# An encoder block: the low part of the gates' token sums made by ScalarE and an accumulating transfer instead of VectorE

## The chip, the cores and the metric

The kernel runs on one core of one Trainium2 chip. The metric is the device time of one execution in microseconds (us); for the kernel before it is the median of the runs that were made. A core has five engines that run their own instruction streams in order and wait for each other through semaphores: TensorE (PE, with its weight loads PEld), VectorE (DVE), ScalarE (ACT), GpSimd (POOL) and SyncE (SP), which here only issues transfers. ACT and POOL can issue transfers too; such an instruction stands in the engine's stream like any other, and what stands behind it waits until it has been issued.

## The reference

One layer of an encoder block works on x, 1024 tokens by 1024 channels, in float32:

```python
u = rms_norm(x, norm1_g[l])
proj = u @ w_in[l]
q, k, v, cb, cc, ch, ga, gb = jnp.split(proj, split_pts, axis=-1)
q = rms_norm(q.reshape(B, S, N_HEADS, HEAD_DIM), q_norm_g[l])
k = rms_norm(k.reshape(B, S, N_HEADS, HEAD_DIM), k_norm_g[l])
y_a = neighbourhood_attention(q, k, v, rpb[l]) @ w_attn_branch[l]
y_b = short_gated_conv(cb, cc, ch, conv_w[l]) @ w_conv_branch[l]
merged = jax.nn.sigmoid(ga) * y_a + jax.nn.sigmoid(gb) * y_b
x = x + merged @ w_o[l]
h = rms_norm(x, norm2_g[l]) @ w_mlp_in[l]
x = x + jnp.square(jax.nn.relu(h)) @ w_mlp_out[l]
```

The gates ga and gb are 1024 channels each. Both are a plain product of u with columns of w_in.

## The kernel before

**Numbers in two parts.** Every operand of a matmul is held as two float16 tiles: a high part, the value rounded to float16, and a low part, the value minus the high part. A product takes three matmuls per 128 rows of contraction (high by high, high by low, low by high), so a unit of 8 contraction blocks is 24 matmuls into one PSUM bank.

**Stages.** The kernel computes in this order: norm of x and the v projection, the q and k projections (token blocks b = 0 to 7 each), attention with the convolution's projections between its steps, the gates and branches, the output projection, and the MLP. The gates after the first block of channels, and the MLP, use a scheme of seven products in place of eight (`seven`): operands are cut into quarters, and some products take sums or differences of quarters. For the gates those sums of the token side ("S forms") are made early, while q is projected, and parked in a DRAM buffer `GS`, to be read back transposed after attention (`turn_s`).

**How the S forms are made (`sforms`, lines 474 to 494).** xt holds the eight blocks of x, normalised in place by two ACT instructions (L482) per pair of blocks n and n+4. Four POOL operations (L486) then make the sums in place, so xt[n] and xt[n+4] become the four forms in float32. This is "form n", for n = 0 to 3. "Split n" follows: a tile s of 128 by 4 by 2 by 512 float16 (three buffers) takes the high part from ACT (L491, 2048 elements in each partition) and the low part from DVE (L493, xt minus the high part). `sform_store` then issues, on ACT's stream (L498), the transfer of the whole tile, 1 MB, to GS. The table `SFORM` sets the order, form 0, 1, 2, split 0, form 3, split 1, 2, 3, each at a mark counted in units of matmuls.

**The order of the work.** It is written out by the program itself: a unit of matmuls is emitted, then foreground generators (`fg`) and background generators (`bg`) are advanced by some steps, and each step emits instructions of DVE, ACT, POOL or SP. So the order within each engine's stream is fixed when the program is built, and on the chip only waits move it.

**What stands around the change.** The v units of blocks 3 to 7 end with an ACT copy (L516) and a DVE operation (L517). A unit of q for block b puts its product into a bank of PSUM taken in turn from tag d (three banks) and tag o (two banks); `qk_vec` then copies it out on ACT (L736), squares it (L737), sums and scales it on DVE (L740, L747), splits it (L754 on ACT, L756 on DVE), and `finish_qk` issues a transpose on SP (L767) into qD. qD takes the place of xt, so the first of these transposes waits for all readers of xt. In the background `Chunk.prep` prepares k's weights: four ACT squares (L266) give a sum, a small matmul (L201) adds it over the partitions, and then ACT makes the high parts (L306) and DVE the low parts (L297) of eight pieces. The units of the k projection need these.

Below, q0 to q7 and k0 to k7 are the units of the q and k projections by block; q0, q2, ... go to banks d, and q1, q3, ... to banks o.

Of the kernel before, what the change touches and what calls it, by code (L numbers as in the profile page):

```python
# [14 lines left out]
AF = mybir.ActivationFunctionType  # L15
OP = mybir.AluOpType
# [36 lines left out]
def encoder_block(ctx: ExitStack, tc: tile.TileContext, x, weights, cols, gqk, rel, masks, out):  # L53
    nc = tc.nc
    V, A, G, T, SP = nc.vector, nc.scalar, nc.gpsimd, nc.tensor, nc.sync
# [41 lines left out]
    def at(c, i, n=1):  # L97
        return slice(c.start + i, c.start + i + n)
# [83 lines left out]
    def apart(mark, n=3, of=units):  # L182
        while of[0] < mark + n and not forced[0]:
            yield WAIT
# [289 lines left out]
    def sforms():  # L474

        for mark, n, split in SFORM:
            yield from apart(mark, 0)
            pair = xt[:, n:n + 5:4]
            if not split:
                assert turned[0] >= n + 5  # L480
                for b in (n, n + 4):
                    A.activation(xt[:, b], xt[:, b], AF.Copy, scale=sc[:, at(ys, b)])  # L482
                z = [xt[:, b, c:c + 512] for b in (n, n + 4) for c in (0, 512)]
                for o, a, b, op in ((3, 2, 3, OP.subtract), (2, 0, 2, OP.subtract),
                                    (0, 3, 0, OP.subtract), (1, 1, 0, OP.add)):
                    G.tensor_tensor(z[o], z[a], z[b], op=op)  # L486
                continue
            v = wqk.tile([128, 4, 2, 512], F16, name="s16", bufs=3)
            v4 = v.rearrange("p (b h) w c -> p b h w c", b=2)
            f = pair.rearrange("p b (h c) -> p b h c", h=2)  # L490
            A.activation(v4[:, :, :, 0], f, AF.Copy)  # L491
            yield
            V.tensor_tensor(v4[:, :, :, 1], f, v4[:, :, :, 0], op=OP.subtract)  # L493
            fg.append(sform_store(n, v))

    def sform_store(n, v):
        yield from apart(units[0], 1)
        A.dma_start(GS[:, n], v)  # L498
        formed[0] = n + 1
# [208 lines left out]
    tick()  # L708
    fg.append(qk_gain())
    fg.append(sforms())  # L710
    step(2)
    for b in range(3, 8):
# [1231 lines left out]
```

## Time and profile before

| | |
|---|---|
| Median of 2 runs | 1206.88 us (1206.52 to 1207.23) |
| Span of the profiled execution, first to last instruction | 1205.3 us |
| PE busy | 1188.0 us, 99% of the span |
| DVE busy | 938.7 us, 78% |
| ACT busy | 759.8 us, 63% |
| POOL busy | 433.1 us, 36% |
| Transfers | 173.36 MB, mean 144 GB/s |

The profiled execution has no time of its own beside its span; what lies between the span and the median of the runs is 1.6 us, before the first and after the last instruction. The span counts from the first instruction. In a timeline each row has its start in us, its length in us, the engine, the source line, the operation, the tile written and the tiles read, the shape, how many instructions the row merges, and in square brackets how long the engine sat idle before it and what ended that. A row of ACTq or SPq is an instruction of the engine's queue, such as the issue of a transfer. In the table of waits the three numbers are the total, the number of times and the longest.

### The profile page before, as it was taken

The numbers are of one execution on the slowest core, as the hardware profiler recorded it, in microseconds if no ns is written. First come the engines' busy times: TensorE is split into PE (matmuls) and PEld (weight loads), VectorE is DVE, ScalarE is ACT, GpSimd is POOL, SyncE is SP. The second block draws the span as 40 slices with busy tenths as digits, with TensorE's granted clock in tenths as the row PEclk, the third lists the DMA queues.
The fourth block names the chain that finished last, engine by engine and source line by source line (L and its number), as shares of the span: only waits on it lengthen the run. The fifth ranks groups of instructions, "written<-read, shape, count | busy, mean of one in ns | idle before, by whom it ended". The sixth has DMA issues, their size and how long they took to land.

```text
span 1205.3 us, 17076 instructions
## 1 busy us (share of the span) xinstructions
PE 1188.0 (99%) x6294; PEld 573.8 (48%) x6294; DVE 938.7 (78%) x1759; ACT 759.8 (63%) x1183; POOL 433.1 (36%) x280
## 2 busy tenths in 40 slices
PE   6999999999999999999999999999999999999998
PEld 4444445555444444444467444444444444444444
DVE  7777988988368787877878655545548999999997
ACT  7766679867554545337779778678676744746440
POOL 1640011222311112001004465565567471553662
PEclk9999999999999999999999999999999999999999
DMA  7766657676542211224386545445465925334202
GB/s 264 151 213 141 140 119 130 133 146 123 103 123 65 67 56 53 70 93 187 57 155 183 182 159 192 149 139 193 145 247 201 352 97 217 129 138 194 105 35 105
DMA packets 171012, 173.36 MB, mean 144 GB/s; under 512 B 131504, under 2 KB 132016, under 8 KB 166832
## 3 DMA queue, kind: packets, MB, share of 16 engines
q1 hardware_dynamic: 170352, 168.07, 47.9%
q10 hardware_dynamic: 576, 4.19, 0.8%
q8 instruction: 49, 0.80, 0.3%
q14 instruction: 35, 0.29, 0.1%
HBM read 102.51 MB, written 37.75 MB: 116 GB/s over the span
## 4 chain that ended last, share of the span: by engine, by line
PE 73%; DVE 9%; ACT 1%; issue 1%; DMA 1%; DVEq 0%; ACTq 0%
PE ps_d L210 26%; PE ps_s L210 23%; PE ps_o L210 16%; PE ps_d L1039 6%; DVE w_s L1163 2%; PE ps_o L1016 1%; PE ps_s L959 1%; DVE sg L1279 1%; DVE P L999 1%; DMA u2T<-v 1%; DVE sz L973 1%; ACT w_s L1167 0%; DVE sc L317 0%; DVE m L1281 0%; ACT sg L1245 0%
## 5 line engine op out<-in xcount | busy, mean ns | idle before, releaser
L210 PEld LDWEIGHTS <-ops 128*128 128x128 f16 x1356 | 132.4, 98 | 157.3
L210 PEld LDWEIGHTS <-w 128*128 128x128 f16 x1368 | 132.8, 98 | 140.0 <-DMA u2T<-v 0.6
L1039 PE MATMUL ps_d<-uT,w_ws 128*128 128x512 f16 x528 | 123.7, 379 | 0.1
L210 PE MATMUL ps_d<-ops 128*128 128x512 f16 (+1 forms) x528 | 118.3, 374 | 0.0
L1765 ACT ACTIVATE ops<-hf,sc 128x2048 f16<-128x2048 f32 x26 | 52.0, 2000 | 97.9 <-PE ps_o L210 35.2
L210 PE MATMUL ps_s<-ops 128*128 128x512 f16 x492 | 112.9, 379 | 0.0
L1152 POOL TENSOR_TENSOR tsum<-raw 128x512 f32<-128x512 f32 x28 | 46.0, 1658 | 149.6 <-ACT raw L1138 141.6
L1345 POOL TENSOR_TENSOR as<-as 128x512 f32<-128x512 f32 x56 | 77.5, 1384 | 39.3 <-ACT as L1625 36.0
L210 PEld LDWEIGHTS <-w_s 128*128 128x128 f16 x588 | 56.8, 98 | 69.4 <-DVE w_s L1163 1.9
L210 PE MATMUL ps_d<-u2x,w 128*128 128x512 f16 (+1 forms) x360 | 80.0, 372 | 0.0
L210 PEld LDWEIGHTS <-uT 128*128 128x128 f16 x504 | 49.0, 98 | 59.6 <-DMA uT<-u 0.8
L1039 PEld LDWEIGHTS <-w_ws 128*128 128x128 f16 x528 | 51.2, 98 | 54.5 <-DVE cv L861 0.4
L210 PE MATMUL ps_o<-ops 128*128 128x512 f16 x336 | 77.1, 379 | 0.0
L1767 DVE SCALAR_TENSOR_TENSOR ops<-hf,sc,ops 128x2048 f16<-128x2048 f32 x26 | 74.0, 2846 | 3.7 <-ACT ops L1765 3.7
L210 PE MATMUL ps_o<-u2T,w 128*128 128x512 f16 (+1 forms) x324 | 71.7, 371 | 0.0
L1138 ACT ACTIVATE raw<-raw,sc 128x256 f32<-128x256 f32 x172 | 71.0, 493 | 0.8 <-DMA raw<-in_weights 0.7
L1152 POOL TENSOR_TENSOR gsum<-raw 128x512 f32<-128x512 f32 x14 | 19.0, 1376 | 133.0 <-issue 72.8
L1167 ACT ACTIVATE w<-raw,sc 128x512 f16<-128x512 f32 (+1 forms) x28 | 24.6, 927 | 54.1 <-DVE sc L426 54.1
L297 DVE SCALAR_TENSOR_TENSOR w_ws<-raw,sc,w_ws 128x512 f16<-128x512 f32 (+2 forms) x72 | 51.2, 763 | 4.7 <-ACT w_ws L306 4.7
L1658 DVE TENSOR_TENSOR as<-ps_d,as 128x512 f32<-128x512 f32 (+1 forms) x14 | 9.4, 672 | 55.8 <-ACT as L1677 53.4
L210 PE MATMUL ps_s<-u2T,w 128*128 128x512 f16 (+1 forms) x252 | 52.7, 359 | 0.0
L982 ACT ACTIVATE sz<-sz,sc 128x384 f32<-128x384 f32 (+1 forms) x64 | 37.2, 582 | 22.5 <-DVE sc L973 15.0
(357 smaller groups left out, 2629.5 us busy)
## 6 DMA issues: line engine op xcount, KB each, us to landing
raw<-in_weights SPq DMA_DIRECT2D x88, 512.0 KB, 5.4
hs<-as SPq DMA_DIRECT2D x16, 1792.0 KB, 8.7
hf<-hs SPq DMA_DIRECT2D x26, 1024.0 KB, 6.3
w2x<-in_weights SPq DMA_DIRECT2D x16, 512.0 KB, 8.1
raw<-in_weights SPq DMA_DIRECT2D x16, 384.0 KB, 3.5
xt<-in_x SPq DMA_DIRECT2D x8, 512.0 KB, 10.0
gs<-s ACTq DMA_DIRECT2D x4, 1024.0 KB, 4.0
x<-in_x SPq DMA_DIRECT2D x8, 512.0 KB, 9.8
```

Source lines behind the costliest of these rows:

```text
L210: T.matmul(ps, l, r, start=a, stop=b)
L297: V.scalar_tensor_tensor(lo, self.raw[p][:, o:o + m], sc[:, c:c + 1], hi, op0=OP.mult, op1=OP.subtract)
L959: T.matmul(ps[:, :nb * 128], QD[:, p, e, w, i * 128:(i + 1) * 128], KD[:, 2 * p + e, lo * 128:(lo + nb) * 128], start=w == 0, stop=w == 1)
L982: A.activation(z, z, AF.Exp, scale=-1.0, bias=sc[:, d["mx"]], accum_out=sc[:, d["sm"]])
L1039: T.matmul(ps, l, r, start=a, stop=b)
L1138: A.activation(v, v, AF.Copy, scale=sc[:, at(g, 4 * i + k)])
L1152: G.tensor_tensor(t[:, o], a, b, op=OP.add)
L1163: V.scalar_tensor_tensor(o(1), w, sc[:, s], o(0), op0=OP.mult, op1=OP.subtract)
L1167: A.activation(o(0), w, AF.Copy, scale=sc[:, s])
L1345: sub.tensor_tensor(z[o], z[a], z[b], op=op)
L1765: A.activation(P[:, 1, 0], hf, AF.Copy, scale=sc[:, Rs])
L1767: V.scalar_tensor_tensor(P[:, 1, 1], hf, sc[:, Rs], P[:, 1, 0], op0=OP.mult, op1=OP.subtract)
```

## The change

The high part is made as before. The low part is no longer a DVE subtraction: ACT writes the negated high part (scale -1) into the place of the low part, and POOL issues two transfers per split, each 128 by 2 by 512 elements, which read the float32 form from xt, convert it, and add it to what stands there.

```diff
             A.activation(v4[:, :, :, 0], f, AF.Copy)
             yield
-            V.tensor_tensor(v4[:, :, :, 1], f, v4[:, :, :, 0], op=OP.subtract)
+            A.activation(v4[:, :, :, 1], v4[:, :, :, 0], AF.Copy, scale=-1.0)
+            for i in range(2):
+                G.dma_start(v4[:, i, :, 1], f[:, i], accum_op=OP.add)
             fg.append(sform_store(n, v))
```

In the changed program the instructions of each engine stand in the order they had, but for these: DVE loses four subtractions; ACT gains four copies, each behind its L491, or behind a later square (for splits 2 and 3); POOL gains eight issues of transfers, two between the sums of form 2 and form 3 (split 0) and six behind form 3 (splits 1, 2 and 3, in this order). The stores of ACT (L498 before) now wait for the two transfers of their split. The first transpose into qD on SP waits for all eight.

The kernel before issues no transfer from POOL.

## The prediction

> **What bounds the kernel now.** I read the page's busy shares first, then the table of who waited for whom on PE.
>
> ```profile
> PE 1188.0 (99%) x6294; PEld 573.8 (48%) x6294; DVE 938.7 (78%) x1759; ACT 759.8 (63%) x1183; POOL 433.1 (36%) x280
> PE ps_o L525 <- ACT u L439: 8.0, 1, 8.0
> PE ps_d L210 <- DVE w_s L1163: 0.2, 1, 0.2
> ```
>
> TensorE is fed nearly without a gap: one wait of 8.0 us at the start, and after it none that matters. So work taken from DVE gains nothing by itself, and a wait that reaches PE costs its full length. The timeline of PE where the splits are made:
>
> ```profile
> 65.40 5.34 PE L210 MATMUL ps_o<-w_ws,uT 128*128 128x512 f16 x24
> 75.76 5.34 PE L210 MATMUL ps_o<-w_ws,uT 128*128 128x512 f16 x24
> 86.12 0.17 PE L201 MATMUL ps_s<-ones 128*128 128x1 bf16 x1
> 86.14 5.34 PE L210 MATMUL ps_o<-w_ws,uT 128*128 128x512 f16 x24
> 101.68 5.34 PE L210 MATMUL ps_d<-w_ws,uT 128*128 128x512 f16 x24
> 106.86 5.34 PE L210 MATMUL ps_o<-w_ws,uT 128*128 128x512 f16 x24
> ```
>
> These are q1, q3, the small sum for k's weights, q5, k0 and k1. A unit takes 5.18 us from start to start. There are two o banks, so q5 (86.14) can't start before ACT has copied out q1. When was that? The timeline of ACT:
>
> ```profile
> 56.98 1.90 ACT L491 ACTIVATE s<-xt 128x2048 f16<-128x2048 f32 x1
> 67.79 0.38 ACTq L498 DMA_DIRECT2D gs<-s  x1
> 68.21 0.60 ACT L516 ACTIVATE vT<-ps_s 128x512 f16<-128x512 f32 x1 [4.49 <-DVE s L493]
> 68.71 1.90 ACT L491 ACTIVATE s<-xt 128x2048 f16<-128x2048 f32 x1
> 71.45 1.06 ACT L266 ACTIVATE w_ws<-raw 128x1024 bf16<-128x1024 f32 x1 [0.84 <-DVE s L493]
> 72.63 1.06 ACT L266 ACTIVATE w_ws<-raw 128x1024 bf16<-128x1024 f32 x1
> 77.41 0.67 ACT L736 ACTIVATE qs<-ps_d,sc 128x512 f32<-128x512 f32 x1
> 78.65 1.04 ACT L266 ACTIVATE w_ws<-raw 128x1024 bf16<-128x1024 f32 x1
> 79.59 0.19 ACT L266 ACTIVATION_READ_ACCUMULATOR w_ws<-raw 128x1 f32 x1
> 80.81 0.34 ACTq L498 DMA_DIRECT2D gs<-s  x1
> 81.19 0.69 ACT L736 ACTIVATE qs<-ps_o,sc 128x512 f32<-128x512 f32 x1 [0.18 <-PE ps_o L210]
> 98.14 2.54 ACT L306 ACTIVATE w_ws<-raw,sc 128x512 f16<-128x512 f32 x4
> ```
>
> Two things are to be seen. First, ACT stands still for its stores: it idled 4.49 us at the store of split 0, which waited for DVE's subtraction. Second, q1 is copied out at 81.19 to 81.88, although PE ended it at 70.7: ACT is already some ten microseconds behind. The slack that is left before PE stops at q5 is 86.14 - 81.88 = 4.26 us. All four stores stand ahead of that copy.
>
> **The change part by part.**
>
> *Removed:* four DVE subtractions, some 10 us.
>
> ```profile
> 64.41 3.35 DVE L493 TENSOR_TENSOR s<-xt,s 128x2048 f16<-128x2048 f32 x1
> 68.28 2.75 DVE L493 TENSOR_TENSOR s<-xt,s 128x2048 f16<-128x2048 f32 x1
> ```
>
> DVE is off the path, so this is worth nothing but for one thing: POOL. The timeline of POOL, its first sum, the first of form 3, and all sixteen:
>
> ```profile
> 44.62 1.27 POOL L486 TENSOR_TENSOR xt<-xt 128x512 f32<-128x512 f32 x1
> 63.90 1.71 POOL L486 TENSOR_TENSOR xt<-xt 128x512 f32<-128x512 f32 x1
> 44.62 30.94 POOL L486 TENSOR_TENSOR xt<-xt 128x512 f32<-128x512 f32 x16
> ```
>
> Form 3 runs from 63.90 to 75.56 (44.62 + 30.94), 11.7 us for four sums, where the first sum took 1.27; it lies exactly beside the subtractions. With them gone I cost form 3 at 4 x 1.27 and three gaps of 0.1 = 5.4 us. If DVE is not the cause it stays 11.7 us: that end is kept, +6.3.
>
> *Added on ACT:* four copies of 2048 elements, float16 to float16, a form that the trace lacks. The same size from float32 took 1.90; I take 1.9. At half of it (cheapest) two copies that lie on the path would give 1.9 back; no row hints at dearer.
>
> *Added on POOL:* eight issues and eight accumulating transfers, neither of which is in the trace. I call D the time from the first issue of a pair until both have landed, and h the time that a pair holds POOL's stream. Nearest rows:
>
> ```profile
> DMA to landing us min/median/max: 3.9/4.0/4.9
> qD<-q SPq DMA_TRANSPOSE x4, 5.0
> 33.43 1.91 SPq L444 DMA_TRANSPOSE uT<-u  x1
> ```
>
> The first row is ACT's store to GS, 1 MB, 4.0 us to landing. One accumulating transfer reads 0.5 MB of float32 and 0.25 MB of float16 and writes 0.25 MB, 1 MB in all. So D is at least one store's 4.0 (both at once, as if free), and at most two of the slowest transfers of this stretch one behind the other, 2 x 5.0 = 10.0. I take two stores one behind the other, D = 8.0. An issue costs between 0.34 (ACT's, above) and 1.91 (a transpose on SP); I take the middle, 1.1, so h = 2.2; at most POOL waits for the first of a pair to land before it issues the second, h = 5.0 + 1.1 = 6.1; at least 0.7.
>
> [...]
>
> *The waits in sequence.* The stores still stand in ACT's stream, now behind transfers that POOL issues behind its sums. Behind each waiting store stand the next split's copy, k's squares and the copies that free PE's banks.
>
> 1. Split 0 is issued when form 2 ends, at 63.90 (its negated copy is done by 60.8: L491 at 56.98 plus two times 1.9). It lands at 71.9. ACT then needs 0.4 + 0.5 + 1.9 (the rows at 67.79, 68.21, 68.71) and is at the second store by 74.7, where it waits again.
> 2. Split 1 is issued behind form 3: 63.90 + h 2.2 + 5.4 = 71.5, landed at T1 = 79.5.
> 3. Split 2: ACT issues the store and makes one square (71.45 to 72.63, 1.2), then the negated copy, 1.9: 3.5 behind T1. Landed at T2 = 79.5 + 3.5 + 8.0 = 91.0. ACT's other work up to the third store (two squares, one L491) fits into that.
> 4. Split 3: store 0.4, q0's copy and square (77.41 to 78.65, 1.24), the last square (78.65 to 79.78, 1.13), the negated copy 1.9: 4.7. Landed at T3 = 91.0 + 4.7 + 8.0 = 103.7.
> 5. The fourth store and q1's copy: 0.38 + 0.69. q1's bank is free at 104.8, against 81.88: 22.9 us late.
>
> So PE waits at q5 for 104.8 - 86.1 = 18.7 us. The small sum ahead of q5 needs the last square, made before T3, and costs nothing more.
>
> *What is late next.* From q1's copy on, ACT and DVE run the same chain as before, so k's weights come 22.9 late, while PE is 18.7 late. Three rows: q2's copy on ACT, the last four low parts of k's weights on DVE, and the first transposes into qD on SP.
>
> ```profile
> 85.06 0.67 ACT L736 ACTIVATE qs<-ps_d,sc 128x512 f32<-128x512 f32 x1
> 102.97 2.68 DVE L297 SCALAR_TENSOR_TENSOR w_ws<-raw,sc,w_ws 128x512 f16<-128x512 f32 x4
> 86.47 8.98 SPq L767 DMA_TRANSPOSE qD<-q  x3
> ```
>
> A q unit takes that chain 3.9 us (81.19 to 85.06), less than PE's 5.18, so it has caught up by k0. The last low part was ready at 105.65 (102.97 + 2.68); k0's 24 matmuls run 0.216 apart and the 23rd needs that part: 101.68 + 22 x 0.216 = 106.43, a slack of 0.78. So PE loses more at k0, up to 22.9 - 0.78 = 22.1 us in all. Behind it the order of lateness is as before, and nothing gives it back: PE has no later wait to absorb it, and every load is issued behind work that shifts too. The first transpose into qD now waits for all eight transfers too (103.7), but q0, its input, comes later still (86.47 + 22.9 = 109.4).
>
> **Sum:** the steps add up to 63.90 + 5.4 + 3.5 + 4.7 + 1.07 + h + 3D = 78.6 + h + 3D for q1's copy; less 81.88 and 0.78 that is h + 3D - 4.1 = 2.2 + 24.0 - 4.1 = **22.1 us**. On the span 1205.3 that is 1227.4; on the median, 1206.88 + 22.1 = **1229.0 us**, 1.8% slower. About 2% (24 us) is what a measurement of this kernel can tell from no change.
>
> **The rivals.**
>
> *Transfers that overlap* (chance 0.25). The second of a pair moves while the first completes. For this: the transfers moved about 400 GB/s during the stores (last column, by stretches of the span).
>
> ```profile
> 70.50:72.50 2.00, 1.92 (x2) 1.00 0.95 397
> ```
>
> A pair reads 1.5 MB, 0.5 more than a store moves, 1.3 us at that rate; with a dearer issue (1.1 for 0.34) D = 4.0 + 1.3 + 0.8 = 6.1. Sum 2.2 + 18.3 - 4.1 = 16.4: 1223 us. Against it: an addition has to read what it adds to first, and 400 GB/s is of plain copies.
>
> *Pairs in strict sequence* (0.27), the other side of 2%. POOL holds its stream until the first of a pair has landed; the kernel reserves only 1024 bytes (`dynamic_dma_scratch_size=1024`) for such transfers. Then each takes 4.0 + 0.76, D = 9.5, h = 4.8 + 1.1 = 5.9, and the sum is 5.9 + 28.5 - 4.1 = 30.3: 1237 us. It crosses 2% where h + 3D passes 28.2. Form 3 staying at 11.7 us leads to the same place (28.4).
>
> *Not slower* (0.02). The accumulations end within the bank's slack. It needs h + 3D under 4.1, so D near 1.1, and then the time is 1207. No landing in this stretch is under 3.9.
>
> *The array comes back slow* (0.08). PE would stand for 18.7 us. Eight transposes near the start and later:
>
> ```profile
> 15.15 1.03 PE L525 MATMUL ps_o<-ident,u 128*128 128x128 f16 x8
> 18.64 0.61 PE L525 MATMUL ps_o<-ident,u 128*128 128x128 f16 x8
> ```
>
> They were slower up to 15 us or so, behind PE's first wait of 8.0. If q5 to q7 ran at half rate as long as at the start (8.0 to 18.64 at most), they would lose 5.3 us. From q1's copy, PE needs 3 x 5.18 + 22 x 0.216 = 20.3 us to k0's 23rd matmul, and the weights need 105.65 - 81.88 = 23.8, so 3.5 of it is hidden and 1.8 reaches the end: 23.9, 1231 us. [...]
>
> **How the numbers follow.** The forecast has 0.36, overlap 0.25, strict sequence 0.27, the slow array 0.08, not slower 0.02, something beyond 0.02. The range goes from D = 4.0 and h = 0.7 (8.6 us, 1216) to D = 10.0 and h = 6.1 (32.0 us, 1239), with a little over for the array: 1216 to 1240. Over 2% slower means above 1231.0: strict sequence nearly whole (0.25), a third of the forecast's own spread (0.12), half of the slow array and what lies beyond (0.06), 0.43. Faster by 2% has 0.01, the rest 0.56.
>
> **What the changed profile would show.** PE's table of waits has one row of some 19 us at L210 for an o bank, released by ACT's copy of qs, and one or several rows of together 3 to 4 us at k0, released by L306 or L297. ACT shows four idle stretches at its stores, each ended by a transfer; the last store stands at 103 to 104 us. The sums of form 3 take some 1.3 us each, begin at 66 and have two issues ahead of them. The stretch behind k0 is as before, only later. The prediction is wrong if a pair lands in 5 us or needs over 10, if ACT's stores don't hold its stream, or if later stages lose or regain microseconds of their own.

## The result, and the profile after

The changed kernel takes **1243.07 us** (two runs, 1242.77 and 1243.36) against 1206.88 before: a ratio of 1.0299 (95% interval 1.0269 to 1.0329), so 36.2 us slower. The prediction was 1229.0 with a range of 1216 to 1240: the sign and the place were right, the size was too small. The profiled execution has a span of 1241.0 us, 35.7 more than before. In the changed kernel the lines behind 493 stand 2 higher (the store is L500, the copy of a q bank L738).

The page's busy shares of the changed kernel:

```profile
PE 1191.6 (96%) x6294; PEld 574.3 (46%) x6294; DVE 926.7 (75%) x1755; ACT 766.9 (62%) x1187; POOL 436.8 (35%) x288
```

DVE lost four instructions and 12 us, ACT gained four and 7 us, POOL gained eight. PE has the same 6294 matmuls and is 3.6 us busier, and it stands still for the rest. Where, the table of waits on PE of the changed kernel says (the total, the number of times, the longest):

```profile
PE ps_s L201 <- DVE ones L272: 18.8, 1, 18.8
PE ps_o L210 <- ACT qs L738: 12.2, 1, 12.2
...
PE ps_d L210 <- DVE w_ws L297: 0.4, 1, 0.4
```

and so does the timeline of PE of the changed kernel:

```profile
80.98 5.34 PE L210 MATMUL ps_d<-w_ws,uT 128*128 128x512 f16 x24
105.15 0.16 PE L201 MATMUL ps_s<-ones 128*128 128x1 bf16 x1 [18.83 <-DVE ones L272]
117.50 8.13 PE L210 MATMUL ps_o<-w_ws,uT 128*128 128x512 f16 x24 [12.18 <-ACT qs L738]
...
139.17 2.58 PE L210 MATMUL ps_d<-w_ws,uT 128*128 128x512 f16 x11 [0.37 <-DVE w_ws L297]
141.58 5.34 PE L210 MATMUL ps_o<-w_ws,uT 128*128 128x512 f16 x24
```

These are q4, the small sum, q5, the second part of k0, and k1. It is one standstill with two names: PE ends q4 at 86.3 and starts q5 at 117.50, where it started at 86.14 before, 31.4 us late. k1 starts 141.58 - 106.86 = 34.7 us late. Behind that, three small steps add 1.0 us up to the end. What they are was not followed up.

The timeline of POOL of the changed kernel has the reason:

```profile
63.83 1.35 POOL L495 DMA_DIRECT2D s<-xt  x1
73.12 1.23 POOL L495 DMA_DIRECT2D s<-xt  x1 [7.95 <-issue]
73.88 5.80 POOL L486 TENSOR_TENSOR xt<-xt 128x512 f32<-128x512 f32 x4
79.63 1.19 POOL L495 DMA_DIRECT2D s<-xt  x1
84.37 1.21 POOL L495 DMA_DIRECT2D s<-xt  x1 [3.55 <-issue]
92.71 1.20 POOL L495 DMA_DIRECT2D s<-xt  x1 [7.12 <-ACT s L493]
97.42 1.21 POOL L495 DMA_DIRECT2D s<-xt  x1 [3.51 <-issue]
107.16 1.20 POOL L495 DMA_DIRECT2D s<-xt  x1 [8.54 <-ACT sc L407]
111.87 1.21 POOL L495 DMA_DIRECT2D s<-xt  x1 [3.50 <-issue]
```

The second transfer of a pair is never issued behind the first: it follows 4.7 us later (79.63 to 84.37, 92.71 to 97.42, 107.16 to 111.87), and 9.3 us later in the first pair. The idle time ahead of it has no releaser ("issue"): it is in the issuing itself. Each time the first transfer has landed some 0.3 us before, as the view of line 495 of the changed kernel shows over all eight:

```profile
DMA to landing us min/median/max: 4.4/4.4/9.0
```

and the list of transfers issued in this stretch (KB each, median us to landing):

```profile
s<-xt POOLq DMA_DIRECT2D x8, 256.0 KB, 4.4
...
bias<-in_rel SPq DMA_DIRECT2D x1, 384.0 KB, 7.8
mk<-in_masks SPq DMA_DIRECT2D x1, 192.0 KB, 6.5
```

The first transfer of all is the one of 9.0. It lies beside SP's loads, and the loads were held up as well. The same two rows of before:

```profile
bias<-in_rel SPq DMA_DIRECT2D x1, 384.0 KB, 4.8
mk<-in_masks SPq DMA_DIRECT2D x1, 192.0 KB, 4.4
```

The timeline of ACT of the changed kernel, where the stores (ACTq L500) wait for the pairs:

```profile
77.63 0.37 ACTq L500 DMA_DIRECT2D gs<-s  x1
...
88.96 0.34 ACTq L500 DMA_DIRECT2D gs<-s  x1
...
90.40 1.89 ACT L493 ACTIVATE s<-s 128x2048 f16<-128x2048 f16 x1
...
101.94 0.34 ACTq L500 DMA_DIRECT2D gs<-s  x1
...
116.38 0.34 ACTq L500 DMA_DIRECT2D gs<-s  x1
116.76 0.69 ACT L738 ACTIVATE qs<-ps_o,sc 128x512 f32<-128x512 f32 x1 [10.15 <-DMA s<-xt]
```

Read with POOL's rows, that is the whole chain: pair 0 holds POOL until form 3 starts at 73.88, form 3 takes 5.8, pair 1 lands at 88.96 (9.3 behind its first issue), 3.75 later pair 2 is issued and takes 9.2, 5.2 later pair 3, and 9.2 later, at 116.38, the last store goes. q1's copy ends at 117.45 in place of 81.88, 35.6 us late.

### The profile page after: what moved, and what is told of

Its sections match the earlier page's. It is cut to its first block, busy times and chain, and to the rows that moved or that the text cites. A ratio compares the mean times of both kernels' runs of the same rounds, so it can differ in the third digit from the quotient of the medians.

```text
span 1241.0 us, 17101 instructions
## 1 busy us (share of the span) xinstructions
PE 1191.6 (96%) x6294; PEld 574.3 (46%) x6294; DVE 926.7 (75%) x1755; ACT 766.9 (62%) x1187; POOL 436.8 (35%) x288
## 4 chain that ended last, share of the span: by engine, by line
PE 71%; DVE 9%; ACT 1%; issue 1%; DMA 1%; DVEq 0%; ACTq 0%
PE ps_d L210 25%; PE ps_s L210 22%; PE ps_o L210 16%; PE ps_d L1041 6%; DVE w_s L1165 2%; PE ps_o L1018 1%; PE ps_s L961 1%; DVE sg L1281 1%; DVE P L1001 1%; DMA u2T<-v 1%; DVE sz L975 1%; ACT w_s L1169 0%; DVE sc L317 0%; DVE m L1283 0%; ACT sg L1247 0%
## 5 line engine op out<-in xcount | busy, mean ns | idle before, releaser
L1767 ACT ACTIVATE ops<-hf,sc 128x2048 f16<-128x2048 f32 x26 | 52.0, 2000 | 98.3 <-PE ps_o L210 35.6
L210 PEld LDWEIGHTS <-uT 128*128 128x128 f16 x504 | 49.7, 99 | 93.4 <-issue 35.7
L210 PE MATMUL ps_o<-w_ws,uT 128*128 128x512 f16 x192 | 45.5, 397 | 12.2 <-ACT qs L738 12.2
```

The costliest lines, as they stand in the source:

```text
L210: T.matmul(ps, l, r, start=a, stop=b)
L1767: A.activation(P[:, 1, 0], hf, AF.Copy, scale=sc[:, Rs])
```

## The experiments

What is to be explained is why a pair holds POOL for 10.0 us and lands after 9.3, and whether the rest of the 36 us is that chain. **The theory:** the 1024 bytes that the program reserves for POOL's transfers hold a single one of this shape, so the second is issued only when the first has landed; the pairs run in strict sequence, and ACT's stream passes this on to PE. **Rivals:** the second is late because an addition itself is slow or has to be over before the next begins; the first use of such transfers has a price of its own; the price is that pair 0 stands in front of form 3; or ACT's four added copies cost more than they seem to. That DVE's operations hold POOL up, as they did with form 3's sums (11.7 us beside the subtractions of before, 5.80 without them), needs no experiment: in the changed kernel's trace DVE ran nothing from 79.4 to 103.7, and two of the holds lie there.

For seven kernels the time follows the start of q1's copy on ACT nearly one to one. (The two with the stores on SP's stream are left out: PE's long wait lies elsewhere there.) The added time is each kernel's median less that of the kernel before on the same chip (1207.66 and 1207.26 us for the two groups of runs, 1206.88 for the changed kernel). What lies ahead of the splits doesn't stand at the same place in every run (q4 starts at 80.94 us in the trace of before, at 79.93 with the copies and DVE's subtraction, at 81.22 with the stores on SP), so no closer agreement is to be expected.

| Kernel | q1's copy starts | later than 81.19 by | added time, us |
|---|---|---|---|
| copies, then DVE's subtraction | 85.20 | 4.0 | 5.2 |
| only split 3 by transfers | 91.65 | 10.5 | 10.6 |
| transfers that don't add | 94.15 | 13.0 | 13.6 |
| one transfer per split | 97.21 | 16.0 | 15.9 |
| room for two transfers | 104.08 | 22.9 | 22.2 |
| the changed kernel | 116.76 | 35.6 | 36.2 |
| all sums first | 117.35 | 36.2 | 36.4 |

### Room for two transfers

```diff
-    sc = base.tile([128, 512], F32, name="sc")
+    sc = base.tile([128, 392], F32, name="sc")
-    area = {"keep": [0, 0, 144], "prep": [144, 144, 240], "tmp": [240, 240, 512]}
+    area = {"keep": [0, 0, 144], "prep": [144, 144, 240], "tmp": [240, 240, 392]}
-    nc = bacc.Bacc(..., dynamic_dma_scratch_size=1024)
+    nc = bacc.Bacc(..., dynamic_dma_scratch_size=2048)
```

> The changed kernel with 2048 bytes in place of 1024 reserved for POOL-issued transfers (and the table of small values sc cut from 512 to 392 columns to make room). Theory A: in the changed kernel POOL holds back the second transfer of each pair until the first has landed because the reserved room takes only one accumulating transfer. Then the second issue (84.37, 97.42, 111.87 there, 4.7 us behind the first) now follows the first within 1.3 us, a pair lands in some 6.8 us in place of 9.3, q1's copy ends near 102 in place of 117.5, and the time is about 1227 us (1223 to 1231). Theory B: accumulating transfers wait for each other whatever room there is: the gaps stay at 4.7 us and the time stays at 1243 us.

Measured: 1229.88 us (1227.53 to 1230.66), 1.018 of before (1.0164 to 1.0195), 13.2 us less than the changed kernel. The timelines of POOL and of ACT with the larger room:

```profile
84.85 2.42 POOL L495 DMA_DIRECT2D s<-xt  x2 [11.12 <-ACT s L493]
96.85 2.44 POOL L495 DMA_DIRECT2D s<-xt  x2 [9.57 <-issue]
```

```profile
91.67 0.34 ACTq L500 DMA_DIRECT2D gs<-s  x1
...
104.08 0.69 ACT L738 ACTIVATE qs<-ps_o,sc 128x512 f32<-128x512 f32 x1 [7.74 <-DMA s<-xt]
```

The two issues of a pair now stand next to each other (x2, some 2.4 us), and a pair with nothing beside it lands in 6.8 us (84.85 to 91.67) where it took 9.2. The smaller table sc changes no instruction: the traces of both kernels list the same ones, in the same order on each engine. So the hold was the room, and the rival that an addition must be over before the next is issued falls. Two transfers at once are not free: one alone lands in 4.4, the second adds 2.4. By slices of 0.3 us the data of such a pair move at some 120 GB/s with hardly a break, from 86.6 to 91.1; in the changed kernel two such stretches of some 2.5 us, of 112 to 133 GB/s, lie apart, so what the room saves is the second one's start, not its moving. With something beside it a pair is still slow: split 1's, issued at 71.30 with loads and then a store under way, needed 9.9 us (its store goes at 81.16).

### Transfers that don't add

```diff
-                G.dma_start(v4[:, i, :, 1], f[:, i], accum_op=OP.add)
+                G.dma_start(v4[:, i, :, 1], f[:, i])
```

> The changed kernel with its eight transfers left plain: they convert xt to float16 and overwrite the negated copy in place of adding to it, so the low part isn't made (the addition is left out). Theory A (room for the reads of an addition): a plain transfer reads one source, so two fit; the second issue follows the first within 1.3 us, a pair lands in 5 to 6 us, the time is about 1222 us (1218 to 1228). Theory B (transfers that POOL issues go one at a time): the second issue still waits for the first's landing, 3.5 to 4.5 us, and the time is 1236 us or more.

Measured: 1221.25 us, 1.0111 (1.0091 to 1.0132). POOL and ACT of this kernel:

```profile
79.02 1.43 POOL L495 DMA_DIRECT2D s<-xt  x2 [7.49 <-ACT s L493]
```

```profile
83.78 0.34 ACTq L500 DMA_DIRECT2D gs<-s  x1
...
94.15 0.69 ACT L738 ACTIVATE qs<-ps_o,sc 128x512 f32<-128x512 f32 x1 [5.70 <-DMA s<-xt]
```

Without the addition both transfers of a pair fit into the same room, an issue takes 0.72 us in place of 1.2, and the pair lands in 4.8 us (79.02 to 83.78). The addition thus costs twice, in room and in moving: 21.8 us against the changed kernel, of which the larger room alone gives back 13.2. A pair of adding transfers is slower than a pair of plain ones where there is room for both (6.8 against 4.8 us); that the read of what is added to is the reason is not shown by these runs.

### One transfer per split

```diff
-            for i in range(2):
-                G.dma_start(v4[:, i, :, 1], f[:, i], accum_op=OP.add)
+            G.dma_start(v4[:, 0, :, 1], f[:, 0], accum_op=OP.add)
```

> The changed kernel with one transfer of each pair left out (the second half of each low part stays the negated high part). Theory: lateness of PE is the chain of four landings on ACT, so with one landing of 4.4 us in place of 9.3 for splits 1 to 3, q1's copy ends near 95 in place of 117.5, PE stands some 9 us at q5, and the time is about 1220 us (1217 to 1224). Rival: the cost is fixed for each split (ACT's copies, hand-overs between POOL and ACT, the first transfer), and the time stays above 1232 us.

Measured: 1223.52 us, 1.013 (1.011 to 1.015), as expected. POOL and ACT of this kernel:

```profile
72.91 1.23 POOL L494 DMA_DIRECT2D s<-xt  x1 [2.71 <-issue]
82.67 1.21 POOL L494 DMA_DIRECT2D s<-xt  x1 [8.52 <-ACT s L493]
```

```profile
87.10 0.34 ACTq L499 DMA_DIRECT2D gs<-s  x1
...
97.21 0.69 ACT L737 ACTIVATE qs<-ps_o,sc 128x512 f32<-128x512 f32 x1 [5.44 <-DMA s<-xt]
```

A single transfer takes 4.4 us from issue to the store behind it (82.67 to 87.10). Even here split 1's transfer was held (72.91): split 0's, issued beside the loads at 63.51, took 9.1 us to land and had the room until then, 72.6.

### The store on SP's stream

```diff
-        A.dma_start(GS[:, n], v)
+        SP.dma_start(GS[:, n], v)
```

> The changed kernel with the four stores to GS issued by SP in place of ACT. Theory: PE stops because ACT's stream stands at the stores. With SP standing there instead, ACT shows no wait for a transfer at q0 and q1, q1's copy ends near 84, and PE passes q5 with at most 1 us of waiting; but the transposes into qD, behind the stores on SP and behind all eight transfers, start near 108 in place of 86.5, the two buffers of q's split run out, and k's weights come some 20 us late: PE stops at k0 for some 18 to 20 us and the time is about 1226 us (1220 to 1231). Rival: the end of the last transfer (116 us) alone sets the lateness, whoever waits for it: 1240 us or more.

Measured: 1234.59 us, 1.0222 (1.0205 to 1.0239), above what was expected. The table of waits on PE, the timelines of ACT and SP:

```profile
PE ps_d L210 <- ACT w_ws L306: 23.1, 1, 23.1
```

```profile
118.88 1.06 ACT L756 ACTIVATE q<-qs 128x1024 f16<-128x1024 f32 x1 [22.41 <-DMA qD<-q]
```

```profile
76.30 34.16 SPq L500 DMA_DIRECT2D gs<-s  x4
```

and that of POOL, where the second of splits 2 and 3 is issued:

```profile
94.61 1.21 POOL L495 DMA_DIRECT2D s<-xt  x1 [5.75 <-issue]
...
105.57 1.21 POOL L495 DMA_DIRECT2D s<-xt  x1 [5.07 <-issue]
```

ACT no longer stands at the stores, and q1's bank is free nearly in time (PE waits 0.4 us at q5). But the stores now stand in SP's stream ahead of the transposes into qD, until 110.46; ACT's next split of a q unit waits 22.4 us for a buffer that a transpose has to read first, and behind it stand the high parts of k's weights (L306). The wait has changed its place and 8.5 of 36 us are won. The expectation had missed what runs beside the transfers: the first ones of splits 2 and 3 were issued 0.2 us behind a store (87.66 and 99.30), and POOL issued the next 7.0 and 6.3 us later, in place of 4.7. The first transpose, behind the last store and two loads on SP, started at 112.02 where 108 was expected, and beside them it was 6.9 us before ACT, which waits for it, went on (118.88); in the kernel before it landed in 4.3. Split 3's copy waited too, 5.1 us for the buffer of split 0, but it was done 13 us before its pair was issued, so this cost nothing.

### ACT's copies alone

```diff
-            for i in range(2):
-                G.dma_start(v4[:, i, :, 1], f[:, i], accum_op=OP.add)
+            V.tensor_tensor(v4[:, :, :, 1], f, v4[:, :, :, 0], op=OP.subtract)
```

The kernel before with the four negated copies added, whose result DVE then overwrites.

> The kernel before with ACT's four negated copies added (VectorE's subtraction then overwrites them; no transfer on POOL). Theory: ACT's copies cost little by themselves, as ACT stood 4.5 us at the first store anyway: two of the four (3.8 us) reach q1's copy, the slack there is 4.3 us and at k's weights 0.8, so 0 to 3 us, 1207 to 1210. Rival: ACT's 7.6 us arrive in full behind the slack, 1213 us or more.

Measured: 1212.44 us, 1.0041 (1.0028 to 1.0054): 5.2 us, more than expected. The timelines of DVE and of ACT:

```profile
81.55 2.29 DVE L494 TENSOR_TENSOR s<-xt,s 128x2048 f16<-128x2048 f32 x1 [5.79 <-ACT s L493]
```

```profile
85.20 0.69 ACT L737 ACTIVATE qs<-ps_o,sc 128x512 f32<-128x512 f32 x1 [0.18 <-issue]
```

Split 3's subtraction now waits for its copy, and ACT in turn for small DVE steps behind that subtraction (3.35 us ahead of L407), before it comes to the store. That puts q1's copy at 85.20, 4.0 us late by the clock of the trace. PE came to this place earlier here than in the trace of before (q4 started at 79.93, before at 75.76 + 5.18 = 80.94), so against PE it is 5.0, 0.7 over the slack of 4.26. That 0.7 is what PE waited at q5, and k's weights cost it further waits at k0. This price is in part one of the form of this experiment (an extra hand-over from ACT to DVE), so it is not to be added to the others.

### Only split 3 by transfers

```diff
+            if n < 3:
+                V.tensor_tensor(v4[:, :, :, 1], f, v4[:, :, :, 0], op=OP.subtract)
+            else:
                 A.activation(v4[:, :, :, 1], v4[:, :, :, 0], AF.Copy, scale=-1.0)
                 for i in range(2):
                     G.dma_start(v4[:, i, :, 1], f[:, i], accum_op=OP.add)
```

> Splits 0 to 2 as in the kernel before (VectorE's subtraction), split 3 alone as changed (negated copy and two accumulating transfers, with no other transfer about). Theory: one pair costs its own landing on ACT's stream. The pair is issued at about 81.7, lands 9.3 later (4.7 to the second issue, 4.6 to its landing), the fourth store stands at 91, q1's copy ends at 92 in place of 81.9, and the time is 9 to 11 us over the kernel before, about 1217 us. If the 9.0 us that the first transfer took in the changed kernel were the price of a first use and not of the loads beside it, the first landing takes 9 here too and the time is about 1221 us. If ACT's standing there did not reach PE, 1208 us.

Measured: 1217.89 us, 1.0084 (1.0071 to 1.0098), as expected. POOL and ACT:

```profile
81.87 1.35 POOL L498 DMA_DIRECT2D s<-xt  x1 [6.61 <-ACT sc L407]
86.72 1.23 POOL L498 DMA_DIRECT2D s<-xt  x1 [3.49 <-issue]
```

```profile
91.65 0.69 ACT L741 ACTIVATE qs<-ps_o,sc 128x512 f32<-128x512 f32 x1 [10.27 <-DMA s<-xt]
```

This pair is the first that the kernel issues. The store stands 0.38 ahead of the copy, at 91.27, so the pair takes 9.4 us, as the later ones of the changed kernel do. The second follows 4.85 us behind the first. The two landed in 4.5 and 4.6 us. So a first use has no price of its own, and the 9.0 us of the changed kernel's first landing belong to its place. One pair alone costs 10.6 us.

### All sums first

```diff
-    SFORM = (..., (9, 2, 0), (9, 0, 1), (10, 3, 0), (10, 1, 1), ...)
+    SFORM = (..., (9, 2, 0), (10, 3, 0), (10, 0, 1), (10, 1, 1), ...)
```

> The changed kernel with form 3 made before split 0 (two entries of the table SFORM exchanged), so that no transfer stands ahead of form 3's sums on POOL and the first transfer is issued near 69.7, when SP's loads are nearly done. Theory of neighbours: the first transfer lands in 4.4 to 5.5 us in place of 9.0, but all eight still go one at a time from 69.7 on, the second split has landed near 88.5 as before, and the time stays within 2 us of the changed kernel's 1243. Theory of first use: the first takes 9 again and the time is 1246 us or more.

Measured: 1243.64 us, 1.0299 (1.0281 to 1.0318), no different from the changed kernel. POOL and ACT:

```profile
69.16 1.34 POOL L495 DMA_DIRECT2D s<-xt  x1
73.97 1.23 POOL L495 DMA_DIRECT2D s<-xt  x1 [3.47 <-issue]
```

```profile
117.35 0.69 ACT L738 ACTIVATE qs<-ps_o,sc 128x512 f32<-128x512 f32 x1 [10.13 <-DMA s<-xt]
```

Form 3 is out of the pairs' way, and the first pair, now five microseconds later and past most of the loads, takes 4.8 to its second issue in place of 9.3. The loads of masks and bias were issued at 64.43 and 64.91, 4.2 us and more ahead of the first transfer; by the 4.4 and 4.8 us of before, an estimate, they were in at 68.8 and 69.7. Nothing is won all the same: form 3 now stands ahead of all eight transfers, where the second one of pair 0 used to move beside it, and the third one, issued just behind the first store, holds the fourth back for 6.3 us in place of 4.7. Which of the two goes first is worth nothing here as long as the eight go one at a time.

### Room for two, and the store on SP

The edits of the first and the fourth experiment together.

> The two edits of ring2k (2048 bytes for POOL's transfers, the table of small values cut to make room) and store_sp (stores on SP) together. Theory: pairs land in 6.8 us, ACT is not held at the stores, and what is left is the first transpose into qD behind the last transfer and store, near 95 in place of 86.5, 8 to 10 us of lateness at k's weights: about 1216 us (1212 to 1220). Rival: the two gains are the same microseconds, and the time stays at ring2k's 1229.

Measured: 1220.32 us, 1.0104 (1.0088 to 1.0119), a little more than expected. The table of waits on PE:

```profile
PE ps_d L210 <- ACT w_ws L306: 8.2, 1, 8.2
```

The two edits take 22.8 us out of the 36, a little over the 13.2 and 8.5 that they gave apart, and of the kernels that add in all four splits with both transfers this is the fastest. It is 13 us slower than the kernel before. No variant tried is faster than that one, and its profile says why: PE waits for DVE 2.5 us in all, and nowhere in the stretch where the splits are made.

POOL's rows of this run also say how much the room holds:

```profile
71.16 3.70 POOL L495 DMA_DIRECT2D s<-xt  x3
75.88 1.19 POOL L495 DMA_DIRECT2D s<-xt  x1 [1.02 <-issue]
```

The view of line 495 of this run gives their landings:

```profile
DMA to landing us min/median/max: 4.5/8.4/9.2
```

The third, fourth and fifth transfers are the row at 71.16, all issued by 74.86, and none of the eight landed in less than 4.5 us, so the third was under way until 75.66 at least. So three were under way at once, and the sixth was held for 1.02 us, until 75.88: 2048 bytes held three such transfers, 1024 held one.

## Why the prediction was wrong, point by point

**What bounds the kernel.** Right. PE lost what the chain on ACT lost, and nothing was won from DVE's 12 us.

**Removed: the subtractions, and form 3.** Right: form 3 takes 5.80 us where 5.4 was worked out and 11.7 was the other end. POOL's sums were slow beside DVE's subtractions and are not any more: in the trace of before, three of form 3's four sums took 3.20, 3.20 and 3.32 us, each beside a subtraction; in the changed kernel DVE ran a single operation of 0.69 us beside the four, which took 5.80 together.

**Added on ACT: copies of 1.9 us.** Right for the duration (1.89, from float16).

**Added on POOL: h = 2.2 and D = 8.0.** This is the step that failed. h was 10.05 (63.83 to 73.88) and D was 9.3, 9.2 and 9.2. D was taken as two stores one behind the other, and h as two issues back to back at 1.1 each. The price of an issue was near (1.2). That two could stand back to back was the error: the room held one. A transfer by itself was 4.4, near the 4.0 of the nearest row. With room for both, D would have been 6.8 where nothing runs beside it, between the forecast and the overlap rival (6.1).

**The sum.** Its form held. With the measured terms, the formula's h + 3D - 4.1 is 10.05 + 27.8 - 4.1 = 33.7; form 3 adds 0.4, and the hand-overs from a store to the next pair 0.7 (3.75 and 5.2 where 3.5 and 4.7 stood): 34.8. k1 was 34.7 late. Of the 12.7 that the sum had been short, h is 7.85, the three D are 3.8, and the rest 1.1.

| Step | predicted | measured |
|---|---|---|
| 1. Split 0 landed | 71.9 | 77.6 |
| 2. Split 1 landed | 79.5 | 88.96 |
| 3. Split 2 landed | 91.0 | 101.94 |
| 4. Split 3 landed | 103.7 | 116.38 |
| 5. q1's bank free | 104.8 | 117.45 |

**The strict-sequence rival** (1237, chance 0.27) named the mechanism and the constant of the program behind it, and the room experiment showed it. It fell short too: it let the first pair hold POOL for 5.9, and the upper end of the range for 6.1, with 5.0 as the slowest landing of the old trace. The pair's first transfer was issued among SP's loads and needed 9.0. That these loads run just there could be seen in the trace of before; no term of the sum and no bound asked what runs beside the new transfers. The upper end of the range had the same hole and ended 3 us below the result. The 5.0 was misread besides: it is the median of four transposes, of which two took 5.6 and 6.0. With 6.0 the range would have gone to 1246 and held the result, but by luck, since no slow transpose was behind it. (Nor is 3.9 the least landing of that stretch, as the rival "not slower" says: loads of weights took 3.5. Nothing in the sum hangs on that.)

**The small sum costs nothing more.** Right in size, but the picture was wrong: the small sum stands in PE's stream ahead of q5 and its last square behind the third store, so the standstill shows as two rows, 18.8 and 12.2, and not as one of 19 at q5.

**What is late next.** The 0.78 of slack at k0 held in the total: 35.6 - 34.7 = 0.9. Of the 3 to 4 us of wait expected there, only 0.4 show as a wait. The rest is in q5, which ran slowly, as the next point says.

**The array comes back slow** (0.08). It did, and it cost nothing. q5's 24 matmuls took 8.13 us in place of 5.34. All 2.8 us lie in time that PE would have waited for k's weights, as that rival's counter-argument had it (3.5 hidden). By stretches of the changed kernel (busy times and counts of PE, PEld, DVE, ACT and POOL, then the granted clock, the transfers' share and GB/s):

```profile
89.00:117.00 28.00, 0.16 (x1) 0.10 (x1) 1.63 (x7) 11.43 (x15) 4.82 (x4) 0.50 0.53 112
117.00:123.00 6.00, 5.50 (x14) 1.93 (x13) 4.02 (x12) 3.63 (x7) 0.00 (x0) 0.50 0.43 175
123.00:130.00 7.00, 7.00 (x33) 3.19 (x32) 5.42 (x17) 4.87 (x8) 0.00 (x0) 0.99 0.82 152
```

**The stretch behind k0 is as before.** Nearly: 1.0 us more was lost behind it.

**The chances.** 0.43 for slower by over 2% and 0.56 for within 2% rested on a forecast in which POOL issues freely. Had the constant of 1024 bytes been read as the likelier case, the sum would have stood at 1237 and on the right side.

## What to carry to other kernels

Before transfers are put on POOL's stream, ask how many of them the room that the program reserves can hold: here only one fitted into 1024 bytes, the issue of the second was a wait for the landing of the first (4.7 us from issue to issue), and everything behind it on that engine waited too (form 3 stood behind pair 0 for 10.0 us). Before a new transfer's time is bounded, look at what else moves at that moment; the longest landing taken from the old trace, 5.0, was no upper end for the 9.0 beside SP's loads. And where the bottleneck engine has no idle time (PE was 99% busy), moving work off a free engine can only be judged by what the new place puts into the chain: the 12 us taken from DVE gained nothing, and the kernel lost 36.2.

## What the runs showed of the hardware

- POOL was held inside an issue, without any releaser in the trace, for 3.5 us and more ahead of the second of a pair when the reserved room was 1024 bytes; with 2048 bytes the same two issues took 2.4 us together, and three transfers were under way at once (three issues in 3.70 us, no landing under 4.5). Of transfers without addition, of the same shape, at least two fitted into 1024 (two issues in 1.43 us).
- An accumulating transfer of 128 x 2 x 512 float32 elements into float16 landed 4.4 us after its issue when quiet and 9.0 us beside SP's loads, which became slower by 2.1 and 3.0 us. DVE's last operation on q's weights ran beside only the first 0.6 us of it, so it can't be the main cause; when the transfer was issued at 69.16, behind most of the loads, the second issue followed 4.8 us behind it, as in a quiet pair (4.7). Where the stores went to SP's stream, the loads of masks and bias stood behind them, and the second issue came after 7.6 us in place of 9.3. Just behind a store it came after 6.3 to 7.0 us in place of 4.7.
- The granted clock was 0.50 from 89 us on, while PE stood still, and stayed so for nearly 6 us after matmuls resumed at 117.50, to 123. From 123 to 130 it was 0.99.
